# A two-layer hybrid decoder trunk: every engine's order made with the timeline model of the program builder

## The chip, the cores and the metric

The kernel runs on one core of a Trainium2 chip. The metric is the device time of one execution in microseconds. A profiled execution has a time of its own, which stands beside the span (first to last instruction) that its trace covers. Five instruction streams matter here: TensorE (PE, with its weight loads PEld), VectorE (DVE), ScalarE (ACT), GpSimd (POOL), and SyncE (SP), which only issues DMAs.

## The reference

A trunk of two layers on x of 256 tokens by 1024 (float32):

```python
for l in range(DEPTH):                      # DEPTH = 2
    mod = (c_act @ ada_w[l] + ada_b[l])     # 9 modulation vectors of 1024
    u = modulate(rmsnorm(x, norm_g[l, 0]), sh1, sc1)
    x = x + 0.5 * (1.0 + g1) * swiglu(u, ffn_w1[l, 0], ffn_w3[l, 0], ffn_w2[l, 0])   # d_ff 2816
    u = modulate(rmsnorm(x, norm_g[l, 1]), sh2, sc2)
    z = u @ w_in[l]                         # 6984 columns
    # four branches: gated linear recurrence, latent attention (MLA),
    # sparse attention with a token indexer (DSA, top 64), complex diagonal state space (S5)
    merged = sum(sigmoid(gate_n) * (y_n @ w_branch[l, n]) for n in range(4))
    x = x + (1.0 + g2) * (merged @ w_out[l])
    u = modulate(rmsnorm(x, norm_g[l, 2]), sh3, sc3)
    x = x + 0.5 * (1.0 + g3) * swiglu(u, ffn_w1[l, 1], ffn_w3[l, 1], ffn_w2[l, 1])
```

## The kernel before

Everything is float32. A large product is made of three matmuls on float32r parts: each operand is split into a high part `hi` (a cast) and a rest `lo`, and the kernel adds hi*hi, hi*lo and lo*hi (`mm3`, L239 to 241, with the tokens stationary; `mm3w`, L244 to 246, with the weights stationary).

A weight tile is an object of class `W` (L216): a DMA on SP's queue brings 128x1024 float32 into a buffer `raw` (L224), ACT casts it to `hi` (L232), DVE subtracts to get `lo` (L233, through the helper at L103), and TensorE then runs 24 matmuls of 256 columns (or 12 of 512) on it. There are five buffers `raw` and four each of `hi` and `lo` (`BUFS`, L67). The split of a tile is traced in `tc.high_priority(offset=PRIO)` with PRIO = 4000, so it goes ahead of what was traced up to 4000 places before it.

The stages of a layer, in the order in which they are traced:

- `start` (L1491), once: norm, modulation and the first products by blocks, as the weights come in.
- `ffn` (L390), the first of the layer: `up_half` (L421) makes 512 columns of w1, then of w3, at a time, `down_proj` (L465) multiplies the 512 columns made before by w2. Between them `step()` advances the preparation of the mixer (`s5_prep`, L621, and others), and each weight tile calls `tick()`, which advances the modulation vectors `ada` (L260) at a rate `RATE`. `ada` brings its matrix in through the same five `raw` buffers and multiplies it on DVE by a per-partition scalar (L275 and the helper at L106), 128x1024 at a time.
- `tail` (L525): the last products, residual, norm and transposes for the next stage, in an order spelled out in `TORD` and traced at `high_priority(offset=TP)`.
- `mixer` (L1368): the four branches, spelled out as 55 steps in the string `ORDER` (L66). Gates (`g`, `gate` L1373) and merges (`p`, `merge` L1384) are large products that need no result of a long chain; the attention steps (`attend` L1093, `mla` L1286, `dsa_index` L1155, `rg_states` L964) are chains of small operations that go between TensorE, ACT, DVE and POOL.
- `tail`, the second `ffn`, `tail` again.

What sets the order: the kernel is traced inside a `tile.TileContext`, and the order in which each engine runs is made when that context closes. The builder plays the traced instructions against a model of the machine. When an engine of the model is free it takes, of the instructions whose inputs (and whose buffer) are ready at that moment of the model, the one that was traced first, `high_priority` counted in. The order so found is written out: each engine's stream is fixed, with semaphore waits between the streams. On the chip nothing is chosen again; an engine whose next instruction has to wait stands still, even where a later one could run. PSUM has eight banks (`bank`, L93 to 96: four `acc`, two `up`, one `tp`, one `ms`).

## Time and profile before

| what | us |
|---|---|
| median of 3 runs | 1520.54 (1517.99 to 1522.41) |
| the profiled execution's own time | 1519.11 |
| its span | 1517.3 |
| PE busy / idle in the span | 1439.0 / 78.3 |
| DVE busy | 1167.0 |
| ACT busy | 771.3 |
| mean granted TensorE clock | 0.982 |

How to read it: a row of the costliest groups or of the timeline names the line, the engine, the operation, the tile written and the tiles read, their shapes, the count, busy time, and in square brackets (or behind the second bar) how long the engine stood idle just before and what ended that. Matmuls are pipelined and overlap in the trace, so the pace of TensorE is read from the distance between the starts of two neighbours and not from one row's duration. PEclk is the granted clock as a share of full speed; 1.00 is 2.4 GHz and 0.50 is 1.2 GHz, and means between them are mixtures.

### The profile page before, as it was taken

To read this page: it belongs to the slowest core of one execution; us is meant where nothing else is said; L and a number is where in the kernel's file an instruction comes from. 1 tells how busy PE (TensorE), PEld (TensorE's weight loads), DVE (VectorE), ACT (ScalarE), POOL (GpSimd) and SP (SyncE) were. 2 spreads that over 40 slices of the span, in tenths; PEclk is the share of its full clock that TensorE was granted. 3 is DMA by queue.
4 is the path that set the end of the run, shared out by engine and by line. 5 is a ranking of instruction groups with operands and counts; after the bars stand their busy time and mean duration, and the time that the engine had idled before them with its cause. 6 is when DMAs were issued, how large, how long until landed. Compare 5 with 4: busy or idle time off the path is not lost.

```text
span 1517.3 us, 26622 instructions
## 1 busy us (share of the span) xinstructions
PE 1439.0 (95%) x10342; PEld 1288.4 (85%) x10342; DVE 1167.0 (77%) x2003; ACT 771.3 (51%) x1223; POOL 63.6 (4%) x75
## 2 busy tenths in 40 slices
PE   8899998899989999999989998999999999999998
PEld 4588887799878897999979897889988889789997
DVE  3699978789787477988787887678987845866655
ACT  4444446644465545444454445467455655544442
POOL 0000000001010000000010000000200100000000
PEclk9999999999999999999999999999999999999999
DMA  9788888786335265899978878754642425567762
GB/s 288 232 294 285 291 258 259 203 232 172 96 102 140 70 206 175 289 320 323 321 250 257 277 244 273 229 135 135 178 132 90 124 83 158 162 212 225 235 207 98
DMA packets 241703, 313.24 MB, mean 206 GB/s; under 512 B 27704, under 2 KB 168872, under 8 KB 241576
## 3 DMA queue, kind: packets, MB, share of 16 engines
q1 hardware_dynamic: 241576, 311.53, 66.0%
q8 instruction: 81, 1.33, 0.4%
q14 instruction: 46, 0.38, 0.1%
HBM read 310.41 MB, written 1.07 MB: 205 GB/s over the span
## 4 chain that ended last, share of the span: by engine, by line
PE 62%; DVE 19%; DMA 7%; issue 5%; ACT 5%; POOL 2%; SPq 0%; POOLq 0%; DVEq 0%; ACTq 0%
DVE lo_genexpr L103 7%; PE ps_up_up_half L244 6%; PE ps_up_up_half L245 6%; PE ps_up_up_half L246 6%; PE ps_acc_down_proj L241 3%; PE ps_acc_down_proj L240 3%; PE ps_acc_down_proj L239 3%; DMA raw_init<-in_ffn_w_dram 3%; DMA raw_ada<-in_ada_w_dram 3%; PE ps_up_gate L244 3%; PE ps_up_gate L246 3%; PE ps_up_gate L245 2%; ACT hi_genexpr L232 2%; PE ps_up_merge L245 2%; PE ps_up_merge L244 2%
## 5 line engine op out<-in xcount | busy, mean ns | idle before, releaser
L232 ACT CAST hi_genexpr<-raw_init 128x1024 fp32r<-128x1024 f32 (+2 forms) x430 | 441.1, 1028 | 504.6 <-DMA raw_init<-in_ffn_w_dram 120.5
L103 DVE TENSOR_TENSOR lo_genexpr<-raw_init,hi_genexpr 128x1024 fp32r<-128x1024 f32 (+2 forms) x430 | 511.5, 1192 | 162.9 <-ACT hi_genexpr L232 155.4
L244 PE MATMUL ps_up_up_half<-uh_new_u,hi_genexpr 128*128 128x256 f32 x1216 | 339.0, 279 | 3.3 <-DVE p_silu_cols L106 2.6
L246 PE MATMUL ps_up_up_half<-uh_new_u,lo_genexpr 128*128 128x256 f32 x1216 | 337.0, 278 | 0.2 <-DVE lo_genexpr L103 0.2
L245 PE MATMUL ps_up_up_half<-ul_new_u,hi_genexpr 128*128 128x256 f32 x1216 | 337.1, 277 | 0.0
L244 PEld LDWEIGHTS ps_up_up_half<-uh_new_u,hi_genexpr 128*128 128x128 f32 x1216 | 228.5, 188 | 9.3 <-issue 7.0
L245 PEld LDWEIGHTS ps_up_up_half<-ul_new_u,hi_genexpr 128*128 128x128 f32 x1216 | 228.5, 188 | 1.4
L246 PEld LDWEIGHTS ps_up_up_half<-uh_new_u,lo_genexpr 128*128 128x128 f32 x1216 | 228.5, 188 | 0.8 <-DVE lo_genexpr L103 0.8
L106 DVE SCALAR_TENSOR_TENSOR acc_ada<-raw_ada,c_col_tile_trunk,acc_ada 128x1024 f32<-128x1024 f32 x105 | 134.4, 1280 | 28.7 <-DMA raw_ada<-in_ada_w_dram 28.3
L244 PE MATMUL ps_up_gate<-uh_new_u,hi_genexpr 128*128 128x256 f32 x512 | 145.3, 284 | 0.0
L245 PE MATMUL ps_up_gate<-ul_new_u,hi_genexpr 128*128 128x256 f32 x512 | 144.1, 281 | 0.0
L246 PE MATMUL ps_up_gate<-uh_new_u,lo_genexpr 128*128 128x256 f32 x512 | 143.6, 281 | 0.0
L239 PE MATMUL ps_acc_down_proj<-hi_genexpr,yT_mul_cols 128*128 128x512 f32 x288 | 115.7, 402 | 0.0
L241 PE MATMUL ps_acc_down_proj<-hi_genexpr,yT_mul_cols 128*128 128x512 f32 x288 | 115.6, 402 | 0.0
L240 PE MATMUL ps_acc_down_proj<-lo_genexpr,yT_mul_cols 128*128 128x512 f32 x288 | 115.3, 401 | 0.1
L244 PEld LDWEIGHTS ps_up_gate<-uh_new_u,hi_genexpr 128*128 128x128 f32 x512 | 96.5, 188 | 2.2 <-issue 1.5
L246 PEld LDWEIGHTS ps_up_gate<-uh_new_u,lo_genexpr 128*128 128x128 f32 x512 | 96.6, 189 | 0.5 <-issue 0.4
L245 PEld LDWEIGHTS ps_up_gate<-ul_new_u,hi_genexpr 128*128 128x128 f32 x512 | 96.5, 188 | 0.1
L239 PEld LDWEIGHTS ps_acc_down_proj<-hi_genexpr,yT_mul_cols 128*128 128x128 f32 x288 | 54.8, 190 | 13.3 <-issue 1.6
L240 PEld LDWEIGHTS ps_acc_down_proj<-lo_genexpr,yT_mul_cols 128*128 128x128 f32 x288 | 54.8, 190 | 12.8 <-DVE lo_genexpr L103 0.6
L241 PEld LDWEIGHTS ps_acc_down_proj<-hi_genexpr,yT_mul_cols 128*128 128x128 f32 x288 | 54.8, 190 | 12.6
L239 PE MATMUL ps_up_tok_gemm<-hi_genexpr,uh_new_u 128*128 128x424 f32 (+2 forms) x88 | 34.0, 386 | 2.2 <-ACT gt_gate L112 2.2
(476 smaller groups left out, 2750.7 us busy)
## 6 DMA issues: line engine op xcount, KB each, us to landing
raw_init<-in_ffn_w_dram SPq DMA_DIRECT2D x240, 512.0 KB
raw_ada<-in_ada_w_dram SPq DMA_DIRECT2D x128, 512.0 KB
raw_init<-in_w_in_dram SPq DMA_DIRECT2D x96, 512.0 KB
raw_init<-in_w_branch_dram SPq DMA_DIRECT2D x32, 512.0 KB
raw_init<-in_ffn_w_dram SPq DMA_DIRECT2D x36, 256.0 KB
raw_init<-in_w_out_dram SPq DMA_DIRECT2D x16, 512.0 KB
s5p_load<-in_ada_w_dram SPq DMA_DIRECT2D x16, 256.0 KB
s5p_load<-in_ada_w_dram SPq DMA_DIRECT2D x8, 512.0 KB
```

The source lines that it names most:

```text
L103: eng.tensor_tensor(o, x, y, op)
L106: V.scalar_tensor_tensor(o, x, s, y, op0, op1)
L232: S.copy(self.hi, self.raw)
L239: T.matmul(o, xh, wh, start=first, stop=False)
L240: T.matmul(o, xh, wl, start=False, stop=False)
L241: T.matmul(o, xl, wh, start=False, stop=last)
L244: T.matmul(o, wh, xh, start=first, stop=False)
L245: T.matmul(o, wh, xl, start=False, stop=False)
L246: T.matmul(o, wl, xh, start=False, stop=last)
```

## The change

The context that traces the kernel is opened with `schedule_with_timeline_sim=True`. The builder then plays the same traced instructions, with the same priorities, buffers and dependences, against its other model of the machine (the timeline model, which follows queues and devices of the core) in place of its default one. An instruction that is ready at a different moment of the model may be taken earlier or later, so every engine's order can come out differently, SP's order of DMAs and the moment at which a buffer is handed on among them. No instruction's shape, type, engine or operand is edited.

```diff
     out = nc.dram_tensor("out_0_dram", (1, 256, D), F32, kind="ExternalOutput").ap()
-    with tile.TileContext(nc) as tc:
+    with tile.TileContext(nc, schedule_with_timeline_sim=True) as tc:
         tile_trunk(tc, args, out)
     r = _run(nc, [arrays], core_ids=[0])
```

## Rows read from the trace of the kernel before

**Rows 1.** The page: busy time, share of the span and instructions of each engine
```profile
PE 1439.0 (95%) x10342; PEld 1288.4 (85%) x10342; DVE 1167.0 (77%) x2003; ACT 771.3 (51%) x1223; POOL 63.6 (4%) x75
```

**Rows 2.** Busy time by stage: start, ffn, mixer, ffn, ffn, mixer, ffn
```profile
core 0: us, PE busy (x) PEld busy (x) DVE busy (x) ACT busy (x) POOL busy (x), PEclk, DMA share, GB/s
0.00:76.00 76.00, 63.97 (x395) 39.57 (x396) 38.60 (x92) 33.05 (x58) 6.48 (x14) 0.93 0.84 260
76.00:237.00 161.00, 156.15 (x1094) 138.79 (x1094) 147.03 (x257) 78.57 (x98) 3.57 (x5) 1.00 0.86 285
...
262.00:585.00 323.00, 304.53 (x2353) 279.11 (x2352) 246.96 (x498) 172.41 (x323) 20.18 (x20) 0.97 0.55 157
...
600.00:781.00 181.00, 178.83 (x1282) 162.44 (x1281) 152.61 (x222) 83.18 (x98) 0.45 (x1) 1.00 0.89 306
...
797.00:985.00 188.00, 180.13 (x1287) 163.03 (x1286) 150.18 (x191) 90.16 (x103) 2.54 (x5) 0.98 0.79 256
...
1000.00:1320.00 320.00, 306.21 (x2348) 285.56 (x2347) 248.47 (x501) 180.97 (x342) 20.11 (x20) 0.98 0.49 140
...
1345.00:1517.00 172.00, 166.62 (x1184) 153.38 (x1182) 103.45 (x106) 70.95 (x78) 0.00 (x0) 1.00 0.63 194
```

**Rows 3.** Timeline of PE inside an ffn: start, duration, line, operation
```profile
702.38 0.28 PE L245 MATMUL ps_up_up_half<-ul_new_u,hi_genexpr 128*128 128x256 f32 x1
702.49 0.28 PE L246 MATMUL ps_up_up_half<-uh_new_u,lo_genexpr 128*128 128x256 f32 x1
```

**Rows 4.** Timeline of PE: the seven long stalls inside ffn and mixer stages
```profile
275.82 0.76 PE L986 MATMUL ps_acc_rg_states<-r_conv,rgw_tile_trunk 128*128 128x256 f32 x1 [2.87 <-DVE r_conv L106]
...
299.18 0.44 PE L300 MATMUL ps_tp_ada<-cst_tile_trunk,mrow_ada 128*128 128x128 f32 x2 [2.62 <-DVE mrow_ada L103]
...
393.43 0.79 PE L1190 MATMUL ps_acc_dsa_index<-dki_dsa_index,s_dsa_index 32*128 32x256 f32 x2 [2.48 <-ACT p_dsa_index L112]
...
433.42 0.64 PE L1346 MATMUL ps_tp_mla<-cst_tile_trunk,s5p_mla 128*96 128x128 f32 x4 [2.59 <-DVE s5p_mla L103]
...
939.62 0.77 PE L759 MATMUL ps_tp_s_prep<-cst_tile_trunk,b_s_prep 128*128 128x128 f32 x4 [2.65 <-ACT s5Cc_s_prep L765]
...
1130.74 1.69 PE L1190 MATMUL ps_acc_dsa_index<-dki_dsa_index,s_dsa_index 32*128 32x256 f32 x4 [2.48 <-ACT p_dsa_index L112]
...
1170.76 0.64 PE L1346 MATMUL ps_tp_mla<-cst_tile_trunk,s5p_mla 128*96 128x128 f32 x4 [2.59 <-DVE s5p_mla L103]
```

**Rows 5.** Busy time by stretch, with the granted clock, around two of the stalls
```profile
380.00:418.00 38.00, 35.02 (x341) 32.89 (x341) 28.93 (x90) 18.58 (x41) 2.69 (x3) 0.91 0.31 92
418.00:456.00 38.00, 33.62 (x212) 28.85 (x210) 31.74 (x76) 24.30 (x49) 4.54 (x2) 0.96 0.33 101
```

**Rows 6.** Timeline of ACT just before the stall that ends at 393.43
```profile
390.84 0.58 ACT L116 COPY s5p_s_out_prep<-ps_acc_s_out_prep 32x64 f32<-32x64 f32 x2 [2.20 <-DVE s5p_s_out_prep L118]
391.32 1.04 ACT L232 CAST hi_genexpr<-raw_init 128x1024 fp32r<-128x1024 f32 x1
392.39 0.36 ACT L116 COPY s5p_s_out_prep<-ps_acc_s_out_prep 32x256 f32<-32x256 f32 x1
392.78 1.57 ACT L112 ACTIVATE p_dsa_index<-ps_acc_dsa_index 128x512 f32<-128x512 f32 x3
```

**Rows 7.** Costliest groups: count, then busy us, mean ns, then idle before
```profile
L103 DVE TENSOR_TENSOR lo_genexpr<-raw_init,hi_genexpr 128x1024 fp32r<-128x1024 f32 (+2 forms) x430 | 511.5, 1192 | 162.9 <-ACT hi_genexpr L232 155.4 <-DMA s_ada<-in_ada_b_dram 2.6 <-PE ps_up_up_half L246 1.1
L232 ACT CAST hi_genexpr<-raw_init 128x1024 fp32r<-128x1024 f32 (+2 forms) x430 | 441.1, 1028 | 504.6 <-DMA raw_init<-in_ffn_w_dram 120.5 <-PE ps_up_up_half L245 111.7 <-PE ps_up_gate L245 65.1
L106 DVE SCALAR_TENSOR_TENSOR acc_ada<-raw_ada,c_col_tile_trunk,acc_ada 128x1024 f32<-128x1024 f32 x105 | 134.4, 1280 | 28.7 <-DMA raw_ada<-in_ada_w_dram 28.3
L112 ACT ACT_TABLE_LOAD x15 | 19.2, 1283 | 1.0 <-PEq L1639 0.7
```

**Rows 8.** Waits of the DMA queue: who for whom, us in total, times, longest
```profile
SPq L224 <- DVE lo_genexpr L103: 587.5, 272, 18.1
```

## Prediction

> **What bounds the kernel now.** I began with the engines' busy times [rows 1]. The reader should see that TensorE is busy 1439.0 of the 1517.3 us of the span, so 78.3 us of it are idle, and that DVE comes second with 1167.0 and ACT third with 771.3. The share is a mean over unlike stages, so I next read the busy times by stage [rows 2]. Four ffn stages (702 us together) hold 681.7 us of PE work: 20.3 us idle. The two mixers (643 us) hold 610.7: 32.3 us idle. The start loses 12.0 of its 76. These three leave 13.7 us for the five stretches of the tails that lie between. In the first ffn DVE is busy 147.0 of 161 us, which is 91%, and in the second 84%; there PE and DVE are close to a tie.
>
> Busy time alone doesn't say that PE runs at its pace, so I looked at the distance of two matmuls' starts inside an ffn: 702.38 to 702.49, 0.11 us for 256 columns [rows 3]. At 2.4 GHz 256 columns take 0.107 us if one enters each cycle, so inside an ffn TensorE takes about a column a cycle and no order of the other engines makes it go faster. The order can only change how long PE stands still, and at which clock it goes on.
>
> Where does it stand still? In the timeline of PE I took every idle stretch of over 2.4 us that lies inside an ffn or a mixer. There are seven [rows 4], and together they are 2.87 + 2.62 + 2.48 + 2.59 + 2.65 + 2.48 + 2.59 = 18.3 us. All seven have one shape: PE's next instruction in its stream belongs to a short chain (a convolution, a modulation vector, the DSA indexer, a transposed MLA key, S5's preparation), and the chain's ACT or DVE step is later than the stream expected. Two of them recur in the second layer with the same length to 0.01 us, so they are made by the order and not by chance. Such a stall costs more than its idle time. The stretch around the one that ends at 393.43 has a granted clock of 0.91 and the one around 433.42 has 0.96 [rows 5]: over 38 us that is 3.4 and 1.5 us of full speed lost. By stage the mixers' clocks are 0.97 and 0.98 and the third ffn's 0.98 [rows 2]: 9.7 + 6.4 + 3.8 = 19.9 us, to the rounding of the clock. So the seven stalls are worth at most 18.3 + 19.9 = 38 us, about 5.5 us each.
>
> **What the change removes, adds and moves.** It edits no operation. What it removes and adds are waits: the streams are laid out anew, so each can wait elsewhere. I go through them by engine.
>
> PE. Matmuls on weights have to follow the weights, and with five `raw` and four `hi` and `lo` buffers no tile can run far ahead, so the large products keep their sequence nearly as traced. What can move is where a chain's small operation is put among them. Put too early, it stops PE (a stall as above, 2.6 us of idle, and up to 3.4 of clock); put too late, the chain runs later, which costs nothing as long as gates and merges are left to fill PE. Bounds per moved place: a gain or a loss of 2.5 to 6.0 us.
>
> ACT and DVE. The stall at 393.43 shows what their order does [rows 6]. ACT stood idle for 2.20 us before a small copy of S5's preparation that had to wait for DVE, then ran a 1.04 us cast for a weight and another copy, and only then the step of the indexer for which PE was waiting. A model that knows better when that copy can start puts the indexer's step first; a model that errs in another place makes the same kind of stall there. The unit of harm on DVE is one product of a modulation vector, 1.28 us, or one weight's rest, 1.19 us [rows 7]. In the ffn stages a step out of turn is covered: a weight tile gives PE 24 x 0.11 = 2.6 us of work and needs 1.19 us of DVE and 1.03 of ACT, and up to four split tiles can stand ready. The cover is thin where DVE is at 91%. If it is gone, each displaced rest costs up to 1.28 us; for a tenth of the 430 rests that is 55 us, so I take 0 and keep 55 us as the upper end.
>
> SP and POOL. SP's queue waits for a `raw` buffer through DVE's rest 272 times, 587.5 us in all [rows 8]. The DMAs therefore follow DVE's order whatever the model says of a DMA, and DMA is no bound in the mixers (shares 0.55 and 0.49) while it reaches 0.89 in the second ffn [rows 2]. A modulation matrix issued ahead of a weight takes one of the five buffers; ACT already waits for weights there (120.5 us in all, [rows 7]), and PE does not, since that ffn is idle for only 2.2 of 181 us. I take 0. POOL is busy 63.6 us; its steps are parts of the chains and are counted with them.
>
> ACT's tables. There are 15 table loads of 1.28 us [rows 7]. Another order of Exp, Tanh, Sin and Sqrt may want more or fewer; ten more would be 12.8 us of an engine at 51%, hidden but for one or two inside a chain. I take 0, with 3 us to either side.
>
> The sum. Forecast: of the seven stalls about three go, because the other model times their chains differently, and about seven others arise, because the chains, buffers and banks are just as tight and the new order meets them afresh; net four more. Why more and not fewer: where the present order puts PE next to a chain, it misses by over 2.4 us only seven times among the 9,548 matmuls of these stages [rows 2, 4], and half of that time (the ffn) stands at 97% busy, so nearly every place that is disturbed can lose and few can win. Four is a choice, between none and a doubling of the seven. At 5.0 us each, between the bounds 2.5 and 6.0 and nearer the latter since a stall took 5.5 on average above, that is +20 us: 1519.1 + 20 = 1539 us on the profiled execution's scale. That one is 1.4 us below the median shown, which I leave in the range.
>
> The Trainium skill's page Perfetto Trace Analysis, section Identifying the Most-Contended Engine, says that matmul busy time is a poor measure of TensorE's headroom and that the busy share of weight loads is the better one. That share is 85% here [rows 1], and it would put 1517.3 - 1288.4 = 229 us within reach of a better order, where the idle time puts 78. The distance of the starts in an ffn [rows 3] speaks for the smaller figure there.
>
> **The rivals.**
>
> *The chains come out right (faster).* The timeline model sees the steps of a chain end later than the default one did, and takes gate products first; PE's stalls in the mixers go. For it: all seven stalls are of the sort "the producer was later than the order assumed", and mixers have idle DMA and ACT (172 of 323 us busy) to bring the filler in. Against it: gates have three `gt` buffers, so not much can be brought forward. All seven away is 1519 - 38 = 1481; half of that is 1519 - 19 = 1500, which is this rival's time. It decides if the new order removes at least one stall more than it makes.
>
> *DVE loses its turn in the ffn (much slower).* Products of modulation vectors, 105 + 15 of them, get in front of weights' rests where DVE is at 91% and 84%. The price is the 55 us above: 1519 + 55 = 1574 us. Against it: the rests are traced at a priority 4000 places higher, and that stays.
>
> *Nothing that counts moves (no change).* Either the two models order alike, or the streams change only where PE is not waiting: 1519 us. For it: large products keep their sequence. Against it: a chain's place depends on a moment of the model, and the attention, indexer and scan chains are full of them, so I think equality unlikely.
>
> **How the numbers follow.** About 0.3% (4.6 us) is what a measurement of this kernel can tell from no change. Chances: forecast 0.42 at 1539 (its own range 1525 to 1558); faster rival 0.35 at 1500 (1481 to 1514); DVE rival 0.08 at 1574 (1558 to 1600); no change 0.15 at 1519. So faster 0.35, within 0.3% 0.15, slower 0.50. The range from 1491 to 1572 leaves out the lowest quarter of the faster case (0.09), about half of the DVE rival (0.04) and a little of the forecast's tail, less than 0.2 together.
>
> **What the profile would show.** If I am right, PE's busy time stays near 1439 us minus what clock does to it, the idle time grows from 78 to about 90 us, the mean granted clock falls below 0.982, and the list of PE's idle stretches over 2.4 us inside ffn and mixer has some eleven entries, at other places than now. If the first rival is right, the entries at the indexer and the MLA key are gone and the mixers' clock is 0.99 or more. If the second, the first ffn takes visibly more than 161 us and PE waits there for `lo_genexpr`. I would be wrong altogether if the sequence of the large products itself changed, say gates and merges in another order, or the tails' stretches grew; nothing in the trace of before prices that.

## The result, and the profile after

The changed kernel takes 1576.8 us (median; 1568.2 to 1583.1) where the kernel before takes 1519.3 us on the same chips: a ratio of 1.037, 95% interval 1.032 to 1.043. It is slower, by 57 us, nearly three times the 20 us that were forecast, and outside the range.

The page of the changed kernel, busy times first, then the chain that ended last by engine:

```profile
PE 1458.7 (93%) x10342; PEld 1311.6 (83%) x10342; DVE 1157.8 (74%) x2003; ACT 769.9 (49%) x1223; POOL 73.2 (5%) x75
...
PE 64%; DMA 15%; DVE 12%; ACT 5%; issue 4%; SPq 1%; POOL 0%; DVEq 0%; ACTq 0%
```

The same chain of the kernel before:

```profile
PE 62%; DVE 19%; DMA 7%; issue 5%; ACT 5%; POOL 2%; SPq 0%; POOLq 0%; DVEq 0%; ACTq 0%
```

The share of transfers (DMA) in it has doubled. The instruction counts of PE, DVE, ACT and POOL are those of [rows 1]. PE's idle time grew from 78.3 to 113.2 us (+34.9), and its busy time, for the same 10,342 matmuls, by 19.7 us, while the mean granted clock fell from 0.982 to 0.954. The two make 54.6 us, the whole difference of the spans (1571.9 - 1517.3). So the loss is PE standing still, and PE going on at a lower clock. The next view says where; it answers to [rows 2] with the tails shown as well:

```profile
core 0: us, PE busy (x) PEld busy (x) DVE busy (x) ACT busy (x) POOL busy (x), PEclk, DMA share, GB/s
0.00:76.00 76.00, 62.69 (x392) 40.86 (x393) 41.08 (x147) 39.28 (x69) 6.41 (x14) 0.91 0.88 257
76.00:237.00 161.00, 155.72 (x1093) 139.77 (x1093) 140.99 (x201) 75.60 (x89) 3.66 (x5) 0.99 0.87 290
237.00:270.00 33.00, 20.50 (x81) 17.14 (x80) 20.93 (x38) 13.58 (x33) 3.23 (x3) 0.74 0.56 162
270.00:597.00 327.00, 305.95 (x2377) 281.05 (x2376) 243.23 (x491) 173.80 (x322) 21.56 (x19) 0.97 0.53 152
597.00:625.00 28.00, 19.25 (x72) 14.21 (x71) 21.20 (x55) 14.50 (x33) 1.87 (x2) 0.76 0.42 132
625.00:800.00 175.00, 175.00 (x1268) 159.98 (x1267) 143.79 (x192) 79.71 (x89) 0.00 (x0) 1.00 0.89 303
800.00:836.00 36.00, 20.93 (x84) 15.82 (x83) 19.90 (x35) 12.27 (x26) 5.48 (x5) 0.76 0.52 153
836.00:1016.00 180.00, 177.62 (x1290) 162.75 (x1289) 149.24 (x192) 86.97 (x101) 4.76 (x5) 1.00 0.82 265
1016.00:1041.00 25.00, 18.45 (x78) 15.43 (x77) 14.82 (x32) 12.57 (x32) 2.74 (x3) 0.81 0.24 64
1041.00:1370.00 329.00, 311.63 (x2310) 291.27 (x2310) 240.45 (x485) 175.33 (x326) 21.53 (x17) 0.93 0.46 132
1370.00:1394.00 24.00, 17.89 (x81) 13.60 (x80) 14.36 (x28) 11.78 (x23) 1.93 (x2) 0.86 0.30 88
1394.00:1571.00 177.00, 173.04 (x1234) 159.75 (x1232) 107.79 (x111) 74.53 (x82) 0.00 (x0) 1.00 0.63 197
```

Read it by kind of stage. The five tails (237, 597, 800, 1016, 1370) take 146 us and PE is idle for 49.0 of them, where the five stretches between the stages of [rows 2], 96 us together, left 13.7. The granted clock is 0.74 to 0.86 there; it was 0.89 to 1.00 before. The mixers are idle for 38.4 us (before 32.3), and the second one's clock is 0.93 (before 0.98). The four ffn stages, 11.6 us idle in 693, are better than before (20.3 in 702): the second holds no idle time at all and the third's clock is 1.00.

The list of PE's long stalls, which [rows 4] gave for the kernel before, is a different one. These are all idle stretches of over 2.4 us after the start (timeline of PE; in brackets the idle time before the instruction and what ended it):

```profile
249.26 0.44 PE L347 MATMUL ps_up_norm_h<-cst_tile_trunk,b_tail 128*128 128x128 f32 x1 [6.81 <-DVE b_tail L344]
...
608.08 0.80 PE L239 MATMUL ps_up_up_proj<-s5p_genexpr,uh_new_u 128*128 128x512 f32 x1 [4.60 <-ACT uh_new_u L366]
...
814.79 0.45 PE L347 MATMUL ps_up_norm_h<-cst_tile_trunk,b_tail 128*128 128x128 f32 x1 [9.84 <-DVE b_tail L344]
...
1026.66 0.71 PE L239 MATMUL ps_up_tok_gemm<-dq_genexpr,uh_new_u 128*128 128x416 f32 x1 [3.83 <-ACT uh_new_u L366]
...
1173.03 0.58 PE L244 MATMUL ps_up_gate<-uh_new_u,hi_genexpr 128*128 128x256 f32 x1 [2.57 <-DVE s5p_merge L106]
...
1378.87 0.80 PE L239 MATMUL ps_up_up_proj<-s5p_genexpr,uh_new_u 128*128 128x512 f32 x1 [4.87 <-ACT uh_new_u L366]
```

None of the seven stalls of before is left. Five of these six lie in the tails, one in each, 30 us together, and wait for the chain residual add, sum of squares, normalised rows (`b_tail`), transposes, next input (`uh`, `ul`). The kernel before has two stalls over 2.4 us in its tails as well, 2.78 us each, which [rows 4] leaves out because it lists ffn and mixers alone. Its third tail, with the transposes and the next input on PE, a modulation product on DVE, and the window:

```profile
782.21 1.07 PE L347 MATMUL ps_up_norm_h<-cst_tile_trunk,b_tail 128*128 128x128 f32 x8 [0.44 <-DVE b_tail L344]
...
786.75 0.80 PE L239 MATMUL ps_up_up_proj<-s5p_genexpr,uh_new_u 128*128 128x512 f32 x1 [2.78 <-ACT uh_new_u L366]
...
777.78 0.75 DVE L275 TENSOR_SCALAR acc_ada<-raw_ada,c_col_tile_trunk 128x1024 f32<-128x1024 f32 x1 [0.18 <-DMA raw_ada<-in_ada_w_dram]
...
781.00:797.00 16.00, 12.78 (x56) 9.19 (x55) 14.83 (x26) 10.95 (x22) 4.46 (x5) 0.89 0.66 197
```

Why is that chain late? The third tail of the changed kernel on DVE, and the two DMA issues that belong to it on SP's queue:

```profile
796.01 2.35 DVE L103 TENSOR_TENSOR lo_genexpr<-raw_init,hi_genexpr 128x1024 fp32r<-128x1024 f32 x2
803.58 0.75 DVE L275 TENSOR_SCALAR acc_ada<-raw_ada,c_col_tile_trunk 128x1024 f32<-128x1024 f32 x1 [5.22 <-DMA raw_ada<-in_ada_w_dram]
804.25 1.28 DVE L103 TENSOR_TENSOR p_add<-ps_acc_down_proj,gt_mod_gate 128x512 f32<-128x512 f32 x2
805.45 1.28 DVE L103 TENSOR_TENSOR X_tile_trunk<-X_tile_trunk,p_add 128x512 f32<-128x512 f32 x2
808.70 1.28 DVE L106 SCALAR_TENSOR_TENSOR acc_ada<-raw_ada,c_col_tile_trunk,acc_ada 128x1024 f32<-128x1024 f32 x1 [1.97 <-DMA raw_ada<-in_ada_w_dram]
...
797.25 0.34 SPq L269 DMA_DIRECT2D raw_ada<-in_ada_w_dram  x1
...
804.36 0.33 SPq L269 DMA_DIRECT2D raw_ada<-in_ada_w_dram  x1
```

The first product of a modulation vector of the next stage stands ahead of the first two residual adds. Its load was issued at 797.25, so the product starts 6.3 us later, at 803.58; DVE stands for 5.22 us of that with the adds behind it. The second product does it again for 1.97 us. The kernel before has the same two products in its third tail, but the first stands behind a residual add and its load has all but landed (0.18 us of waiting at 777.78), and the second doesn't wait. In all, the product's group waits for its loads for 65.3 us, against 28.3 before [rows 7], and its first form for another 13.9 (before 1.4):

```profile
L106 DVE SCALAR_TENSOR_TENSOR acc_ada<-raw_ada,c_col_tile_trunk,acc_ada 128x1024 f32<-128x1024 f32 x105 | 134.6, 1281 | 65.7 <-DMA raw_ada<-in_ada_w_dram 65.3
L275 DVE TENSOR_SCALAR acc_ada<-raw_ada,c_col_tile_trunk 128x1024 f32<-128x1024 f32 x15 | 11.2, 749 | 13.9 <-DMA raw_ada<-in_ada_w_dram 13.9
```

The Trainium skill's page PSUM — Partial Sum Buffer, section Engine vs sequencer instructions, says that the queues of ScalarE, VectorE and GpSimdE are strict FIFO. The trace agrees: nothing overtakes the product that waits at 803.58.

In the mixers the picture is another one. Windows in the second mixer, then PE's attention steps in the middle one:

```profile
1241.00:1272.00 31.00, 31.00 (x251) 28.41 (x250) 17.96 (x33) 15.72 (x29) 3.85 (x2) 1.00 0.46 135
1272.00:1300.00 28.00, 23.12 (x119) 19.09 (x117) 9.63 (x21) 14.00 (x42) 0.00 (x0) 0.71 0.15 41
1300.00:1320.00 20.00, 15.69 (x86) 14.16 (x85) 4.85 (x9) 6.67 (x15) 0.00 (x0) 0.67 0.16 52
...
1274.35 1.10 PE L1121 MATMUL ps_ms_attend<-dc_dsa_in,p_attend 128*128 128x64 f32 x8 [1.06 <-ACT p_attend L116]
...
1280.98 1.11 PE L1133 MATMUL ps_tp_y_trans<-cst_tile_trunk,p_attend 128*128 128x128 f32 x4 [0.79 <-DVE p_attend L103]
...
1285.81 1.97 PE L1121 MATMUL ps_ms_attend<-dc_dsa_in,p_attend 128*128 128x64 f32 x8 [0.73 <-ACT p_attend L116]
```

From 1241 to 1272 gate products lie between the steps of the attentions, PE is never idle and the clock is 1.00. Then no gate product runs until 1327, where the last 96 of this mixer's 768 follow. Attention steps, and some merges, follow each other with waits of 0.5 to 1.1 us and one of 2.4, and the clock falls to 0.71 and 0.67: 48 us that hold 38.8 of PE work, much of it at the lower level. The kernel before still lays gate products between the same steps, in its second mixer from 1228 to 1266:

```profile
1228.00:1266.00 38.00, 37.87 (x278) 33.48 (x278) 15.98 (x30) 22.80 (x60) 0.00 (x0) 1.00 0.26 71
```

The traces give the count. In each mixer of both kernels 480 gate products stand ahead of the first of the 144 matmuls of attention transposes and values. Of the next ones, the kernel before lays 93 among the first three eighths of these matmuls and 93 among the rest; the changed kernel lays 192 among the first three eighths and none among the rest.

### The profile page after: what moved, and what is told of

It is laid out like the page before. It is cut to its first block, busy times and chain, and to the rows that moved or that the text cites. A ratio compares the mean times of both kernels' runs of the same rounds, so it can differ in the third digit from the quotient of the medians.

```text
span 1571.9 us, 26653 instructions
## 1 busy us (share of the span) xinstructions
PE 1458.7 (93%) x10342; PEld 1311.6 (83%) x10342; DVE 1157.8 (74%) x2003; ACT 769.9 (49%) x1223; POOL 73.2 (5%) x75
## 4 chain that ended last, share of the span: by engine, by line
PE 64%; DMA 15%; DVE 12%; ACT 5%; issue 4%; SPq 1%; POOL 0%; DVEq 0%; ACTq 0%
DMA raw_ada<-in_ada_w_dram 9%; PE ps_up_up_half L244 5%; PE ps_up_up_half L246 5%; PE ps_up_up_half L245 5%; DVE lo_genexpr L103 4%; PE ps_up_gate L244 4%; PE ps_up_gate L245 4%; PE ps_up_gate L246 4%; DMA raw_init<-in_ffn_w_dram 3%; PE ps_acc_down_proj L240 3%; PE ps_acc_down_proj L239 3%; PE ps_acc_down_proj L241 3%; PE ps_up_merge L244 2%; PE ps_up_merge L245 2%; PE ps_up_merge L246 2%
## 5 line engine op out<-in xcount | busy, mean ns | idle before, releaser
L106 DVE SCALAR_TENSOR_TENSOR acc_ada<-raw_ada,c_col_tile_trunk,acc_ada 128x1024 f32<-128x1024 f32 x105 | 134.6, 1281 | 65.7 <-DMA raw_ada<-in_ada_w_dram 65.3
L241 PE MATMUL ps_acc_down_proj<-hi_genexpr,yT_mul_cols 128*128 128x512 f32 x288 | 114.2, 397 | 0.0
L239 PE MATMUL ps_acc_down_proj<-hi_genexpr,yT_mul_cols 128*128 128x512 f32 x288 | 113.5, 397 | 0.0
L335 POOL TENSOR_TENSOR nrs_norm_rs<-nss_tail,mhalf_tile_trunk 128x1 f32<-128x1 f32 x10 | 10.3, 1027 | 666.6 <-DVE nss_tail L106 666.6
```

Of the source, the lines that this page charges most:

```text
L106: V.scalar_tensor_tensor(o, x, s, y, op0, op1)
L239: T.matmul(o, xh, wh, start=first, stop=False)
L241: T.matmul(o, xl, wh, start=False, stop=last)
L335: G.tensor_tensor(rs, ss, mhalf[:, 0:1], OP.pow)
```

## The experiments

Most kernels use one method: in a chosen stretch, chosen engines are given the order that the other of the two kernels has there (as a rule the changed kernel gets the order of before), by edges that fix the order on one engine and add no wait between engines; the scheduler of the kernel orders the rest. Its core, where `names` is the whole order of one engine in the other kernel, `lo` and `hi` bound the stretch in it, and `order(then, first)` adds an edge (the last two loops keep the `k` neighbours on either side outside the stretch):

```diff
+def pin(tc, stretches, k=250):
+    ...
+    for s, lo, hi in stretches:
+        names = [n for n in unpack(s) if n in at]
+        inside = names[lo:hi]
+        for first, then in zip(inside, inside[1:]):
+            order(then, first)
+        for n in names[max(0, lo - k):lo]:
+            order(inside[0], n)
+        for n in names[hi:hi + k]:
+            order(n, inside[-1])
...
         tile_trunk(tc, args, out)
+        pin(tc, PINS)
```

The table holds every run. "Loss" is worked out from each profiled execution: for two consecutive matmuls, the distance of their starts less the distance that such a pair keeps in the kernel before when unhindered (the 15th percentile there), summed over a kind of stage. It counts idle time and low clock together, and doesn't depend on which stage a matmul was moved to. Stages that have the same order in several kernels differ by 1 to 5 us between these executions, and a profiled execution lies up to 6 us from its kernel's median, so losses and times agree no better than that. How the loss divides also depends on where a stage ends: by the windows shown above the tails grew by 50 us (96 to 146) and the mixers by 13 (643 to 656), where the table has 42 and 26. The times of the kernels don't depend on that.

| kernel | put back, or ruled | time, us | ratio to before | loss: tails | mixers | start, ffn |
|---|---|---|---|---|---|---|
| before | | 1519.3 | 1 | 27.6 | 106.0 | 86.7 |
| changed | nothing | 1576.8 | 1.037 [1.032, 1.043] | 69.5 | 132.5 | 75.4 |
| e1_tails | tails, four engines | 1533.4 | 1.008 [1.004, 1.013] | 29.0 | 138.8 | 69.9 |
| e1_mixers | mixers, four engines | 1542.9 | 1.014 [1.012, 1.016] | 66.0 | 105.2 | 73.7 |
| e1_ffns | ffn, four engines | 1587.9 | 1.045 [1.041, 1.049] | 57.7 | 137.6 | 96.6 |
| e1_tails_mixers | tails and mixers | 1510.2 | 0.992 [0.989, 0.995] | 27.2 | 105.8 | 81.0 |
| e2_ada_behind | rule: products behind tails | 1568.2 | 1.031 [1.027, 1.035] | 50.5 | 143.6 | 78.6 |
| e2_tails_dve | tails, VectorE | 1564.2 | 1.028 [1.022, 1.033] | 54.7 | 147.8 | 69.9 |
| e2_tails_pe | tails, TensorE | 1565.1 | 1.030 [1.026, 1.034] | 51.4 | 130.4 | 86.5 |
| e2_mix_pe | mixers, TensorE | 1551.2 | 1.020 [1.016, 1.023] | 67.8 | 111.0 | 74.0 |
| e3_nowait | nothing; no wait for products' loads | 1554.1 | 1.022 [1.017, 1.026] | 55.7 | 130.2 | 75.4 |
| e3_tails_da | tails, VectorE and ScalarE | 1551.4 | 1.021 [1.016, 1.025] | 46.4 | 140.3 | 74.1 |
| e3_rev_tails | before, with the new tails | 1565.2 | 1.029 [1.027, 1.032] | 76.5 | 100.4 | 85.3 |
| e3_ffn34 | before, with the new 3rd and 4th ffn | 1510.6 | 0.992 [0.989, 0.995] | 31.1 | 106.6 | 76.1 |
| e4_gates | rule: gates not earlier | 1553.7 | 1.020 [1.014, 1.025] | 67.3 | 116.8 | 75.2 |
| e4_mix_da | mixers, VectorE and ScalarE | 1596.1 | 1.047 [1.042, 1.053] | 64.9 | 158.9 | 70.7 |
| e4_ada_pe_mix | rule, and TensorE in tails and mixers | 1526.3 | 1.004 [1.001, 1.007] | 42.9 | 106.4 | 74.4 |

**Which stages.** The first four kernels put back all four compute engines by kind of stage; the start is put back together with the ffn stages.

> The changed kernel, with the instructions of TensorE, VectorE, ScalarE and GpSimd inside the five tails (from the first residual add to the last split of the next stage's input) put back into the order that they had before; everything else stays in the timeline model's order. Theory 1 (a stage's loss is made by the order inside that stage): the tails grew by 29.9 us in the trace, so the time falls from 1577 to about 1547. Theory 2 (the loss is made by what reaches a stage late, the DMA issues above all, which are not put back): the tails stay long, 1570 to 1577. Theory 3 (what the tails give back is lost again in the next stage): also above 1565, but with short tails in the trace.

> The same for the two mixers: the order of before inside them on the same four engines, the timeline model's in the tails and the ffn stages. Theory 1: the mixers grew by 25.0 us, so about 1552. Theory 2: 1570 to 1577.

> The same for the four ffn stages: the order of before inside them, the timeline model's in the tails and the mixers. Theory 1: the ffn stages changed by -0.3 us in all, so 1577 within 0.5%. The rival of the prediction in which VectorE loses its turn in the ffn: these stages hold the loss, so well below, 1530 to 1545.

> Tails and mixers both put back, so that the timeline model's order is left in the ffn stages alone (and on the DMA issues). Theory 1: the two parts add, 1577 - 30 - 25 = 1522, the time before. Theory 3 (a saving in one place is lost in the next): 1545 or more. If the ffn stages gain by themselves (the third one was 5.9 us shorter in the trace), 1515.

Measured: 1533, 1543, 1588 and 1510 us. Put back, the tails return 43 us and the mixers 34 us, so the loss is made by the order inside them, though the DMA issues were left to the model: theory 2 falls. Theory 1 had the places right and the sizes too small, by 13 and 9 us. In the ffn stages (with the start) the timeline model's order is the better one: with the old order there the kernel is 11 us slower still, and with the new order there alone (`e1_tails_mixers`) it is 10 us faster than the kernel before. The rival in which VectorE loses its turn in the ffn is refuted. Theory 3 holds in small: the two savings make 77 us by themselves and 67 together.

**What in the tails.** Two causes could be read from the trace: modulation products ahead of the adds on VectorE, and transposes behind all matmuls of the second token block on TensorE (none of those is left to follow the transposes at 814.79, where in the kernel before three follow the ones at 782.21). `e2_ada_behind` has a rule in place of the pins, in `ada`, where `tail_end` holds VectorE's instructions of the last tail:

```diff
+    def behind(i):
+        for t in tail_end:
+            tc.add_manual_dep(i.ins, t.name, ...)
...
-                stt(acc, raw, c_col[:, k:k + 1], acc, OP.mult, OP.add)
+                behind(V.scalar_tensor_tensor(acc, raw, c_col[:, k:k + 1], acc, OP.mult, OP.add))
```

> The changed kernel, with one ordering rule added: no modulation product (acc_ada) of the next stage may stand before an instruction of the tail on VectorE. The timeline model orders all the rest. Theory 1a (VectorE stands in front of loads of raw_ada that have not landed, with the residual adds queued behind): in the trace it stood 25 us there in the tails 1 to 3, and these three grew by 21.6 us; they go back to 50 us, the time to about 1550, and the fourth tail, which has no such product in it, stays at 16 us. Theory 1b (TensorE's own order: the transposes of the normalised rows stand behind all products of the second token block): the tails stay within 3 us of the changed kernel's and the time above 1570.

> VectorE alone put back into the order of before inside the five tails; TensorE, ScalarE and GpSimd stay in the timeline model's order. Theory 1a: the tails 1 to 3 go back, 1545 to 1555. Theory 1b: above 1570.

> TensorE alone put back into the order of before inside the five tails; VectorE keeps the modulation products ahead of the residual adds. Theory 1a: no more than the fourth tail's 6.9 us come back, 1568 to 1577. Theory 1b: the 44 us that all four engines together gave in the tails come back, about 1535.

Measured: 1568, 1564 and 1565 us. Neither theory is right alone. The rule took 20 us of loss out of the first three tails (50.1 to 29.8) and nothing out of the fourth, as theory 1a said, but the time fell by 9 us only, to 1568 and not to the 1550 expected: the model then laid the first mixer out anew, whose loss rose from 66 to 83 us. In the eight kernels whose first mixer was left to the model it is 66 to 83 us; in the seven with the old order of all four engines or of TensorE there, 55 to 60. TensorE's order alone took 18 us of loss out of the tails and the time fell by 12. What else holds the tails with TensorE put back is seen in the fourth. ACT, and what PE waits for, in `e2_tails_pe`:

```profile
1025.74 1.49 ACT L112 ACTIVATE b_tail<-ps_up_norm_h,mcol_ada,mA_mod_scale_shift 128x128 f32<-128x128 f32 x4
1027.11 0.89 ACT L232 CAST hi_genexpr<-raw_init 128x832 fp32r<-128x832 f32 x1
1027.88 0.63 ACT L366 CAST uh_new_u<-b_tail 128x512 fp32r<-128x512 f32 x1
1028.40 0.90 ACT L232 CAST hi_genexpr<-raw_init 128x832 fp32r<-128x832 f32 x1
1029.19 0.63 ACT L366 CAST uh_new_u<-b_tail 128x512 fp32r<-128x512 f32 x1
...
1029.87 0.46 PE L239 MATMUL ps_up_tok_gemm<-dq_genexpr,uh_new_u 128*128 128x416 f32 x1 [1.85 <-ACT uh_new_u L366]
...
1032.48 0.71 PE L241 MATMUL ps_up_tok_gemm<-dq_genexpr,ul_new_u 128*128 128x416 f32 x1 [1.96 <-DVE ul_new_u L103]
```

and in `e1_tails`, where all engines have the old order:

```profile
992.18 1.49 ACT L112 ACTIVATE b_tail<-ps_up_norm_h,mcol_ada,mA_mod_scale_shift 128x128 f32<-128x128 f32 x4
993.55 1.14 ACT L366 CAST uh_new_u<-b_tail 128x512 fp32r<-128x512 f32 x2
994.58 1.68 ACT L232 CAST hi_genexpr<-raw_init 128x832 fp32r<-128x832 f32 x2
...
994.75 0.46 PE L239 MATMUL ps_up_tok_gemm<-dq_genexpr,uh_new_u 128*128 128x416 f32 x1 [1.01 <-ACT uh_new_u L366]
...
996.33 0.45 PE L241 MATMUL ps_up_tok_gemm<-dq_genexpr,ul_new_u 128*128 128x416 f32 x1 [0.93 <-DVE ul_new_u L103]
```

The timeline model's order sets two casts of the next weights (`hi_genexpr`) between the steps that make `uh`, each 0.9 us, and PE waits 1.85 and 1.96 us instead of 1.01 and 0.93. That is a third displacement, on ScalarE and, with the rests, on VectorE. The next three kernels bear on the three. `e3_nowait` keeps the changed kernel's order of every engine and leaves out the first products' reading of their loads:

```diff
+            elif k < 5 and (l, j) in ((0, 6), (0, 8), (1, 4)):
+                x, acc8 = bc(cst[:, None, 0:128], (128, 8, 128)), acc.rearrange("p (a b) -> p a b", a=8)
+                ...
+                    stt(acc8, x, c_col[:, k:k + 1], acc8, OP.mult, OP.add)
```

> Every engine's order, the DMA issues' too, is exactly that of the changed kernel. The first products (at most five) of the modulation vector that follows each of the tails 1, 2 and 3 read a resident constant instead of their load, so that VectorE does the same work at the same place but doesn't wait there; these three modulation vectors are wrong by that. Theory 1a (the wait for the load is the cost): the three tails lose about as little as with the ordering rule, 19 us less than the changed kernel, about 1558. Theory 1d (VectorE's work is the cost: 13 products of 0.75 to 1.28 us ahead of the adds are 16 us by themselves): 1572 or more.

> VectorE and ScalarE put back into the order of before inside the five tails, TensorE and GpSimd in the timeline model's order. With VectorE alone it was 1564, with TensorE alone 1565, with all four 1533. Theory 1c (three displacements in series: products ahead of adds on VectorE, weight splits between the steps of the chain on ScalarE and VectorE, transposes behind the products on TensorE): TensorE's share stays, 1545 to 1555. Theory 1e (TensorE's order only follows the late chain and costs nothing once the chain is in time): about 1535.

> The kernel before, in the default model's order everywhere but in the five tails, where TensorE, VectorE, ScalarE and GpSimd take the timeline model's order. If the order inside the tails is the cause by itself, it costs here what it cost there: the changed kernel's tails lose 42 us more on TensorE, so about 1520 + 42 = 1562. If the cost hung on what the timeline model does elsewhere (the loads' issue, the mixers), under 1540.

Measured: 1554, 1551 and 1565 us. Without the wait, in the same order, the kernel is 23 us faster by the medians and 17 by the two profiled executions, of which 15 lie in the first three tails (50.1 to 34.8). In the third tail of that kernel neither product waits, the first add waits for PE alone, and PE's stall is 3.39 us instead of 9.84:

```profile
794.47 1.29 DVE L103 TENSOR_TENSOR p_add<-ps_acc_down_proj,gt_mod_gate 128x512 f32<-128x512 f32 x2 [1.65 <-PE ps_acc_down_proj L241]
...
796.87 1.28 DVE L106 SCALAR_TENSOR_TENSOR acc_ada<-cst_tile_trunk,c_col_tile_trunk,acc_ada 128x1024 f32<-128x1024 f32 x1
...
802.96 1.93 PE L353 MATMUL ps_up_norm_h<-cst_tile_trunk,b_tail 128*128 128x128 f32 x8 [3.39 <-DVE b_tail L350]
```

So most of the harm that products do in the tails, 15 of the 20 us that the rule took out, is the wait for their loads and not their 1.28 us each. One thing more went out with the reading: such a product no longer holds its buffer, so SP can fill that buffer again sooner, and the 23 us are for both. With VectorE and ScalarE put back, 25 us return and TensorE's share stays (1551, theory 1c); ScalarE was not put back by itself. The tails' order by itself costs as much in the kernel before: 45 us, with 49 us more loss in the tails and none elsewhere.

**What in the mixers.** TensorE's order alone, then the gates alone, then the other two engines alone. In `e4_gates` each gate product may not be taken before the last attention step that stood ahead of it in the kernel before:

```diff
+    for g, x in zip(unpack(gate), unpack(after)):
+        tc.add_manual_dep(at["I-%d" % g], "I-%d" % x, ns, reason="hold")
```

> TensorE alone put back into the order of before inside the two mixers; the other three engines stay in the timeline model's order there. Theory 2a (the gate products are spent early, between steps of chains that were ready anyway, and the attention steps later run back to back with nothing between them): TensorE's order is the cause, so all of the 34 us that four engines gave come back, about 1543. Theory 2b (VectorE's or ScalarE's order makes the attention chain itself slower): less than a third, above 1565.

> The changed kernel with one rule for TensorE in the mixers: a gate product may not stand earlier, against the attention steps (scores, transposes, values), than it stood in the kernel before. The timeline model orders all the rest, the merges too. Theory 2a (the gates are spent early and nothing is left to lay between the attention steps): most of the 26 us that TensorE's whole order of before gave, about 1555. If other parts of TensorE's order in the mixers matter (merges, recurrences, the index), 1570 or more.

> VectorE and ScalarE put back into the order of before inside the two mixers, TensorE and GpSimd in the timeline model's order. All four engines gave 34 us there, TensorE alone 26. Theory 2a: 1565 or more. Theory 2b (the attention chain is slow because of the order on VectorE and ScalarE, and TensorE's order only follows it): 1550 or less.

Measured: 1551, 1554 and 1596 us. The gates alone give back 23 us where TensorE's whole order gives 26, and the intervals don't tell the two apart: theory 2a. TensorE's order is not all, for the four engines gave 34 and theory 2a had expected that much of TensorE (1543 us). Putting back VectorE and ScalarE under the model's order on TensorE makes the kernel 19 us slower. PE's waits in that kernel (in total, times, longest) show where:

```profile
PE ps_acc_dsa_index L1190 <- ACT p_dsa_index L112: 12.7, 2, 6.9
PE ps_tp_attend L1118 <- ACT p_attend L112: 8.7, 10, 1.7
```

PE stands for up to 6.9 us at the indexer, where it stood for 2.48 in the kernel before [rows 4]: the orders of the engines fit each other. These two engines' order, taken from the other plan, was worse than either whole plan in the mixers (1596 against 1577 and 1543), while TensorE's, taken alone, was better than the new one.

**Do the causes add?**

> The changed kernel with the rule that keeps modulation products behind the tails on VectorE, and TensorE put back into the order of before inside tails and mixers; ScalarE, GpSimd and the rest of VectorE stay in the timeline model's order. If the causes add: from 1577 the rule's loss in the tails 19, TensorE's in the tails 18, TensorE's in the mixers 26, so 1514. If the weight splits between the steps of the tail's chain hold the tails by themselves, some 10 us of that stay: 1524. If a saving at one place is lost at another, above 1535.

Measured: 1526 us. The three put right together give back 51 of the 57 us. The tails keep 43 us of loss against 28 before, so some 15 us stay there, and the 12 us less in start and ffn offset most of them. The weight splits between the steps of the chain were expected to leave some 10 us; they were not tried by themselves, so that the 15 are theirs is not shown.

**A version that beats both.** The timeline model's order is worth having in the ffn.

> The kernel before with the timeline model's order in the third and the fourth ffn stage alone (same four engines). In the runs with tails and mixers put back the third stage was 9 to 13 us shorter than before and the fourth 2 us, so about 1509. If those gains were made by the stages ahead of them and not by the order inside, 1520.

Measured: 1510.6 us, 0.8% faster than the kernel before, and `e1_tails_mixers` is as fast. The third ffn of `e3_ffn34`, in the window of [rows 2], where the kernel before had 180.13 us of PE work at 0.98:

```profile
797.00:985.00 188.00, 186.07 (x1330) 169.24 (x1329) 155.47 (x203) 89.69 (x107) 5.77 (x7) 1.00 0.81 263
```

The stall of 2.65 us at S5's preparation [rows 4] is gone and the clock stays at 1.00.

## Why the prediction was wrong

**What bounds the kernel**: right. The whole difference of the spans is PE's idle time (+34.9 us) and PE's busy time (+19.7). The latter did not stay near 1439 but rose for equal work, as the mean granted clock fell from 0.982 to 0.954.

**The count of stalls**: wrong. That "about three go" and "about seven others arise" was a guess at seven places. All seven went, and one new stall of over 2.4 us arose in the mixers, none in the ffn. By the prediction's own price of 5.5 us a stall, six fewer would have been a gain of 33 us. So that the kernel got slower, as forecast, is luck: the +20 us were made of something that didn't happen. The faster rival's two events came true, the stalls went and gate products were taken first, but not its sign: the mixers' clock is 0.97 and 0.93 and not 0.99 or more. What was gained lies in the ffn stages, 10 us.

**The failed step, first part: the tails.** The prediction put 13.7 us of idle time into them, priced them at nothing, and named their growth among the signs of being wrong altogether, with the remark that nothing in the trace prices it. That was the wrong answer to a question it had asked itself. A tail is a chain over four engines (DVE, ACT, POOL for one small step, PE) with PE waiting at its end, and there is little else for PE to do; the trace of before prices each foreign instruction in it: a product is 1.28 us, a rest 1.19 and a cast 1.03 [rows 7]. The tails lost 42 us more (27.6 to 69.5), some 34 of it idle and the rest by the lower clock; put back, they returned 43.

**The failed step, second part: the DMAs "follow DVE's order whatever the model says of a DMA", with 0 taken for them.** The kernels in which four engines are put back and SP is left alone fit the sentence itself. The converse was left out: DVE's order also comes from the moment at which the model holds a load for landed (inferred, see below), and DVE then stands before a product whose load hasn't landed, in the tails with the chain behind it. In the whole kernel such waits are 79 us (65.3 + 13.9) against 30. The wait was there to be priced: 28.3 us over 105 products [rows 7]. Taken away around the first three tails, it gave 23 us.

**The failed step, third part: a chain put late "costs nothing as long as gates and merges are left to fill PE".** The condition failed, and with it the premise that the large products keep their sequence nearly as traced. Gates were taken earlier, which was written down as part of the faster rival, and so they were gone when the attentions needed something between their steps: 192 among the first three eighths and none behind, where it had been 93 and 93. The mixers lost 26 us more by the table, some 8 of it idle and the rest by the lower clock, and holding the gates back returned 23. The stall's price of 5.5 us, idle and clock about equal, fits neither place: in the tails idle outweighs the clock by some four to one, in the mixers the clock outweighs the idle time by some two to one.

**DVE in the ffn**, taken as 0 with 55 us as the upper end: 0 was right. The ffn stages got faster.

**ACT's tables**, taken as 0: right, 15 loads and 19.2 us as in [rows 7].

The Trainium skill's page Perfetto Trace Analysis, section Identifying the Most-Contended Engine, by which the weight loads' busy share shows TensorE's headroom, was set against the idle time. The share fell from 85% to 83% as the kernel got slower, and the best two kernels, 10 us faster, have 85% and 86%. No run here came near the 229 us that the prediction's estimate from that share would offer.

**What stays open.** That the timeline model takes the loads for landed earlier than they are is inferred: its order puts a product ahead of adds, and the scheduler takes what is ready. No run shows it. Nor is it settled why the first mixer's loss varies by 17 us among kernels that leave it to the model, or what in VectorE's and ScalarE's order makes up the 8 us of the mixers that TensorE's order alone does not return.

## What to carry to other kernels

When the order is what changes, price the places where PE waits at the end of a chain and has nothing else to do, and ask of each engine in the chain which foreign instruction could stand in front of it, and what that one waits for. Filler work is a stock: an order that spends it where the chains are short lacks it where they are long. A scheduler can be chosen by stage: here one model was better in the ffn stages and the other in tails and mixers, and the mixture beat both.

## What was not expected of the hardware

The clock fell without any long stall. From 1272 to 1300 PE is busy for 23.12 of 28 us and no pause is longer than 1.06 us, yet the granted clock is 0.71; eight products `ps_ms_attend`, which take 1.10 us together at 1274.35, take 1.97 at 1285.81. With gate products laid between such steps, from 1241 to 1272, it is 1.00. The prediction had read a lower clock only around stops of over 2.4 us. In the 20 us that follow, at 0.67, one pause is nearly that long: 2.39 us.

The Trainium skill's page TensorE: Matmul & The Clock Gate, section A second HAM failure mode: psum-queue depth-cycling, tells of a kernel in which short idle times between groups of matmuls made the clock go back and forth between its two levels. This trace agrees in kind: eight such products take 1.10 us at 1274.35, 1.97 at 1278.23 and 1285.81 and 1.06 at 1290.56, and no pause between these is longer than 0.79 us.
